# Two-layer hybrid trunk: another order of the projections in the first half of layer 0

## The chip, the cores and the metric

The kernel runs on one core of one Trainium2 chip. The metric is the device time of one execution in microseconds. Engines are named as the profile names them: PE is TensorE (matmuls; PEld its weight loads), DVE is VectorE, ACT is ScalarE, POOL is GpSimd, and SP issues nearly all the DMAs.

## The reference

Two layers run over 2048 prompt tokens and over 8 sample sequences of 16 tokens. Each layer normalises and modulates its input, projects it once into six groups of 512 columns, sends `u` through a state-space branch and `q`, `k`, `v` through stick-breaking attention, gates both branches with SiLU (`z_s`, `z_a`), and projects the joined result onto the residual:

```python
h = rms_norm(x, norm_g) * (1.0 + scale[:, None]) + shift[:, None]
u, z_s, q, k, v, z_a = jnp.split(h @ w_in, [...], axis=-1)
y_s, hr, hi = s5_branch(u, h0_re, h0_im, a_re, a_im, log_dt, ...)   # scan over tokens
y_s = gelu(y_s); y_s = y_s * sigmoid(y_s @ w_glu + b_glu) * silu(z_s)
q = rms_norm(q, q_norm_g); k = rms_norm(k, k_norm_g)                 # per head of 64
y_a = stick_breaking(q, k, v) * silu(z_a)
x = x + gate * (concatenate([y_s, y_a]) @ w_out)
```

Everything is float32. Nothing in the reference orders the six column groups among each other.

## The kernel before

**Tiling.** The 2176 tokens are 17 tiles of 128. They go through a layer in two halves (`TILES`, nine tiles and eight). `proj_half` opens a half: three pairs of buffers `hH`, `hL` hold its normalised input, split into a rounded part and a remainder. `project(st, groups)` then works through column groups one after the other. For each group `weights` loads eight chunks `wr` of 128x512, rounds each on ACT into `wH` (L171) and subtracts the rest into `wL`, on POOL for even chunks and on DVE for odd ones (L172). There are eight `wH` and eight `wL` buffers, so the chunks of one group take the places of the group before it.

**The groups differ in what stands behind PE.**
- `zs` and `za`, the gates, are computed transposed: 12 PSUM tiles `pm` of 128x384, each of 24 matmuls (L726 to L728). A tile leaves through one ACT sigmoid and one DVE product (L731, one operand in PSUM).
- `u`, `v`, `q`, `k` go token tile by token tile: 24 matmuls of 512 columns (L673 to L675) into one `pm`, of which there are two.
- A tile of `q` or `k` goes on through `qk`: two ACT passes, then 16 DVE rows: a sum of squares (L689), twelve narrow steps of 128x8 or so for an inverse root (L194 to L201, all from SBUF to SBUF), a product over 512 columns (L692), then a PE transpose (L696) and the split into `x2` buffers (L706 on ACT, L707 on DVE), which DMAs store to `qT` or `kT`. For `k`, POOL also scales the tile (L698).
- A tile of `v` is stored, read back shifted by one token and subtracted on POOL (L771).

`kn` (three buffers) and `x2` (two) serve all of these; `norm` loads the next half's input into `x2` as well.

**The set-up of the state-space branch** stands between the groups. `ssm_mats(l)` builds matrices in eight batches: on POOL `Gt` (L555), `Et` (L550), `EE` (L552), on DVE `EE` (L551), `GG` (L556, L557), on PE small products (L563) and transposes of `GG` (L573). `ssm_phase(l)` builds a table of rotations by doubling, with DVE and POOL in turn (L444 to L449, L416 to L419). In the first half of layer 0 the chain is `ssm_mats(0)`, both phases, `ssm_mats(1)`, then `ssm_sample(0)`, a serial recurrence on DVE (L1130 to L1133). Each of them takes its buffers from the memory that the one ahead has left, so they follow each other.

**What sets the order.** `build` emits the work in the order of the code. A scheduler then interleaves the instructions of all engines, with earlier emitted work ahead where it is ready by its own estimate of time. The result is one fixed order for each engine and for SP's queue: an instruction that isn't ready holds all that stand behind it on its engine.

Of the kernel before, what the change touches and what calls it, by code (L numbers as in the profile page):

```python
# [44 lines left out]
class Trunk:  # L45
# [6 lines left out]
    def build(self):  # L52
        tc, nc = self.tc, self.nc
        with ExitStack() as es:
# [7 lines left out]
            with ExitStack() as pe:  # L62
                with ExitStack() as px:
# [8 lines left out]
                    st = self.proj_open(pe, 0, 0)  # L72
                    with tc.high_priority(offset=300):
                        self.project(st, ("u",))
                self.project(st, ('q',))
                with ExitStack() as pq:
                    self.stats(self.pool(pq, "stats1", right=True), TILES[1])
                self.ssm_mats(0)
# [2 lines left out]
                    self.ssm_phase(ph, 1)  # L81
                self.ssm_mats(1)
                self.ssm_sample(0)
                self.project(st, ('k', 'v', 'za', 'zs'))
                self.proj_half(st, 1)
                self.project(st, ("u",))
                self.ssm(0)
# [7 lines left out]
            with ExitStack() as pe:  # L95
                st = self.proj_open(pe, 1, 0)
# [5 lines left out]
            with ExitStack() as pe:  # L102
                st = self.proj_open(pe, 1, 1)
# [1180 lines left out]
```

## Time and profile before

| | us |
|---|---|
| median of 3 runs | 3248.16 |
| lowest, highest | 3246.58, 3252.23 |
| the profiled execution | 3246.12 |
| its span, first instruction to last | 3244.3 |

The page of the profile covers the span; 1.8 us of the profiled execution lie around it. Busy time is a union over each engine. Times inside the span count from its start. The stretch that the change touches lies from about 137 us (end of `u`) to 617 us (end of `u` of the second half).

### The profile page before, as it was taken

What the parts mean: (1) busy time and instruction counts of PE and PEld (TensorE: products, weight loads), DVE (VectorE), ACT (ScalarE), POOL (GpSimd) and SP (SyncE); (2) the same over time, 40 slices, a digit from 0 to 9 for tenths busy, and PEclk for the clock granted to TensorE, in tenths of its full rate; (3) what the DMA queues carried; (4) which work ended last, traced back from release to release, by engine and by line L of the source; (5) the groups of instructions that cost most, each with busy time, mean ns of one, the idle gap of its engine ahead of it and who ended that gap; (6) DMA issues with size and microseconds to landing.
All of it is one profiled execution on the core that took longest, in us unless ns stands there. A gap on an engine that the chain in (4) does not pass through costs nothing.

```text
span 3244.3 us, 47167 instructions
## 1 busy us (share of the span) xinstructions
PE 2986.9 (92%) x16902; PEld 2241.4 (69%) x16902; DVE 2233.9 (69%) x3885; ACT 1297.7 (40%) x2646; POOL 710.9 (22%) x468
## 2 busy tenths in 40 slices
PE   6977679899988999999999997899999899999998
PEld 4755578798767657667777785677789565666665
DVE  6699775667476786577885637437474988776865
ACT  4632224334342343365443323463343345343422
POOL 1155664101302022111021003312200202111210
PEclk7999799999999999999999998999999999999999
DMA  6645554465776974343344224757754847444642
GB/s 201 171 145 170 204 174 154 145 184 176 235 267 224 314 228 144 124 139 119 112 139 155 100 65 155 240 193 218 222 173 139 264 127 203 140 129 138 208 136 73
DMA packets 516099, 555.27 MB, mean 171 GB/s; under 512 B 87203, under 2 KB 369491, under 8 KB 515098
## 3 DMA queue, kind: packets, MB, share of 16 engines
q1 hardware_dynamic: 515866, 552.26, 54.3%
q8 instruction: 134, 2.20, 0.3%
q14 instruction: 99, 0.81, 0.1%
HBM read 378.12 MB, written 169.86 MB: 169 GB/s over the span
## 4 chain that ended last, share of the span: by engine, by line
PE 68%; DVE 10%; DMA 5%; issue 4%; ACT 1%; POOL 1%; SPq 1%; DVEq 0%; ACTq 0%; POOLq 0%
PE pt L836 8%; PE po L842 8%; PE pm L673 5%; PE pm L674 5%; PE pm L675 5%; PE pz L819 4%; PE pm L726 3%; PE pz L820 3%; PE pm L728 3%; PE pm L727 3%; PE pm L1243 3%; PE pm L1244 3%; PE pm L1245 3%; DVE u L826 2%; PE pz L990 1%
## 5 line engine op out<-in xcount | busy, mean ns | idle before, releaser
L826 DVE TENSOR_TENSOR_SCAN u<-u 128x512 f32<-128x512 f32 (+3 forms) x640 | 724.2, 1165 | 96.0 <-ACT u L824 92.5
L673 PE MATMUL pm<-wH,hH 128*128 128x512 f32 x1088 | 448.1, 413 | 28.5 <-ACT kn L760 16.3
L674 PE MATMUL pm<-wL,hH 128*128 128x512 f32 x1088 | 444.5, 409 | 10.7 <-DVE wL L172 6.8
L675 PE MATMUL pm<-wH,hL 128*128 128x512 f32 x1088 | 446.4, 411 | 5.9 <-POOL hL L649 4.3
L839 ACT COPY aT<-pt 128x512 f32<-128x512 f32 (+1 forms) x376 | 175.3, 470 | 592.5 <-PE pt L836 568.1
L836 PEld LDWEIGHTS pt<-ident,u 128*128 128x128 f32 x2176 | 240.8, 142 | 233.8 <-issue 194.6
L824 ACT ACTIVATE u<-pz 128x512 f32<-128x512 f32 (+3 forms) x640 | 320.9, 536 | 176.8 <-PE pz L820 61.1
L838 DVE COPY aT<-pt 128x512 f32<-128x512 f32 (+1 forms) x376 | 199.6, 534 | 250.9 <-PE pt L836 241.0
L836 PE MATMUL pt<-ident,u 128*128 128x128 f32 x2176 | 350.8, 285 | 15.5 <-DVE aT L838 11.3
L842 PE MATMUL po<-aT,V 128*64 128x512 f32 (+1 forms) x1504 | 318.4, 506 | 16.4 <-DVE aT L838 7.7
L819 PE MATMUL pz<-K,Q 128*128 128x512 f32 (+2 forms) x640 | 271.6, 425 | 4.8 <-issue 1.6
L726 PE MATMUL pm<-hH,wH 128*128 128x384 f32 (+1 forms) x768 | 259.8, 338 | 17.5 <-DVE kn L731 17.5
L728 PE MATMUL pm<-hH,wL 128*128 128x384 f32 (+1 forms) x768 | 257.3, 336 | 11.0 <-POOL wL L172 8.8
L673 PEld LDWEIGHTS pm<-wH,hH 128*128 128x128 f32 x1088 | 210.6, 194 | 78.9 <-ACT kn L760 17.7
L727 PE MATMUL pm<-hL,wH 128*128 128x384 f32 (+1 forms) x768 | 258.0, 336 | 0.0
L674 PEld LDWEIGHTS pm<-wL,hH 128*128 128x128 f32 x1088 | 210.4, 193 | 60.7 <-DVE wL L172 9.8
L675 PEld LDWEIGHTS pm<-wH,hL 128*128 128x128 f32 x1088 | 210.6, 194 | 58.1 <-POOL hL L649 8.0
L172 POOL TENSOR_TENSOR wL<-wr,wH 128x512 fp32r<-128x512 f32 x96 | 152.3, 1597 | 415.4 <-ACT wH L171 217.3
L820 PE MATMUL pz<-K,Q 128*128 128x512 f32 (+2 forms) x640 | 235.3, 368 | 0.0
L1243 PE MATMUL pm<-owH,mH 128*128 128x512 f32 x512 | 207.4, 405 | 10.0 <-DVE yt L1246 8.8
L1244 PE MATMUL pm<-owL,mH 128*128 128x512 f32 x512 | 205.0, 400 | 4.6 <-DVE owL L172 4.5
L1245 PE MATMUL pm<-owH,mL 128*128 128x512 f32 x512 | 203.6, 398 | 0.0
(373 smaller groups left out, 5211.7 us busy)
## 6 DMA issues: line engine op xcount, KB each, us to landing
wr<-in_w_in_dram SPq DMA_DIRECT2D x192, 256.0 KB
K<-kT SPq DMA_DIRECT2D x184, 256.0 KB
Q<-qT SPq DMA_DIRECT2D x112, 256.0 KB
wm<-in_w_mod_dram SPq DMA_DIRECT2D x24, 1024.0 KB
V<-dv_d SPq DMA_DIRECT2D x92, 256.0 KB
out_dram<-kn SPq DMA_DIRECT2D x68, 256.0 KB
qT<-x SPq DMA_DIRECT2D x64, 256.0 KB
kT<-x SPq DMA_DIRECT2D x64, 256.0 KB
```

What stands on the lines that cost most here:

```text
L673: pe.matmul(ps, hH[:, k, cs], wH[k], start=k == 0, stop=False)
L674: pe.matmul(ps, hH[:, k, cs], wL[k], start=False, stop=False)
L675: pe.matmul(ps, hL[:, k, cs], wH[k], start=False, stop=k == KT - 1)
L726: pe.matmul(ps[:, 0:n], wH[k][:, ws], hH[:, k, 0:n], start=k == 0, stop=False)
L727: pe.matmul(ps[:, 0:n], wH[k][:, ws], hL[:, k, 0:n], start=False, stop=False)
L728: pe.matmul(ps[:, 0:n], wL[k][:, ws], hH[:, k, 0:n], start=False, stop=k == KT - 1)
L819: pe.matmul(pz[:, c0:512], Q1[:, qi], K1[:, 0:N], start=True, stop=False)
L820: pe.matmul(pz[:, c0:512], Q2[:, qi], K1[:, 0:N], start=False, stop=not diag)
L824: sc.activation(u[:, o:512], pz[:, c0:c1], AF.Sigmoid, scale=-0.125)
L826: v.tensor_tensor_scan(un, un, un, 1.0 if diag else carry[hh * 4 + i], ALU.mult, ALU.bypass)
L836: pe.transpose(pTs[hh][:, i * 128:(i + 1) * 128], As[hh][i][:, off + j * 128:off + (j + 1) * 128], ident)
L842: mm = pe.matmul(po[c, s], V1[:, j, c], aTs[hh][:, s], start=diag and j == 0, stop=kc == 0 and j == 3, tile_position=(0, hh * 64))
```

## The change

Two lines of `build` change. In the first half of layer 0 the groups are emitted as `u`, `zs`, `za`, (set-up), `v`, `k`, `q` where they were `u`, `q`, (set-up), `k`, `v`, `za`, `zs`. The number of instructions of each kind stays.

```diff
                     with tc.high_priority(offset=300):
                         self.project(st, ("u",))
-                self.project(st, ('q',))
+                self.project(st, ('zs', 'za'))
                 with ExitStack() as pq:
                     self.stats(self.pool(pq, "stats1", right=True), TILES[1])
                 self.ssm_mats(0)
@@
                 self.ssm_mats(1)
                 self.ssm_sample(0)
-                self.project(st, ('k', 'v', 'za', 'zs'))
+                self.project(st, ('v', 'k', 'q'))
                 self.proj_half(st, 1)
                 self.project(st, ("u",))
```

The scheduler makes of it another order on every engine. On DVE, in the middle of `ssm_mats(0)`, the order before has the normalisation of `q` and `k` (L200, L201, L689) between the set-up's rows:

```order
L556 TENSOR_TENSOR GG_2128<-PWT_1973,Bb1_1982 128x1024
L200 TENSOR_TENSOR rst_1920<-rst_1920,rsm_1919 128x8
L567 TENSOR_TENSOR KK_2139<-KK_2139,Dd_2047 128x16
L557 TENSOR_TENSOR GG_2128<-GG_2128,Gt_2129 128x1024
L201 SCALAR_TENSOR_TENSOR rrq_1918<-rst_1920,rrq_1918 128x8
L551 TENSOR_TENSOR EE_2193<-PWT_1973,C2_1997 128x1088
L689 TENSOR_REDUCE ssq_3118<-x1_3114 128x8
```

The same place of the change, on DVE, has the products of the gate `za` (L731) there:

```order
L551 TENSOR_TENSOR EE_2384<-PWT_2199,C2_2223 128x1088
L567 TENSOR_TENSOR KK_2330<-KK_2330,Dd_2273 128x16
L731 TENSOR_TENSOR kn_1840<-pm_1815,kn_1840 128x384
L731 TENSOR_TENSOR kn_1869<-pm_1844,kn_1869 128x384
L556 TENSOR_TENSOR GG_2354<-PWT_2199,Bb1_2208 128x1024
L551 TENSOR_TENSOR EE_2419<-PWT_2199,C2_2223 128x1088
```

Between the first and the last `EE` or `GG` row of `ssm_mats(0)` DVE had 186 rows of `qk`; now it has none, and 19 products of the gates.

In the middle of `ssm_mats(1)`, on DVE, the order before has gate products and weight remainders:

```order
L557 TENSOR_TENSOR GG_2585<-GG_2585,Gt_2586 128x1024
L551 TENSOR_TENSOR EE_2650<-PWT_2465,C2_2489 128x1088
L731 TENSOR_TENSOR kn_4340<-pm_4315,kn_4340 128x384
L567 TENSOR_TENSOR KK_2596<-KK_2596,Dd_2539 128x16
L172 TENSOR_TENSOR wL_4384<-wr_4381,wH_4383 128x512
L556 TENSOR_TENSOR GG_2620<-PWT_2465,Bb1_2474 128x1024
```

The same place of the change, on DVE, has the normalisation of `k` (two tiles in turn):

```order
L692 TENSOR_TENSOR kn_4049<-kn_4049,rrq_4054 128x512
L199 TENSOR_TENSOR rst_4117<-rrq_4115 128x8
L557 TENSOR_TENSOR GG_2846<-GG_2846,Gt_2847 128x1024
L200 TENSOR_TENSOR rst_4117<-rst_4117,rsm_4116 128x8
L551 TENSOR_TENSOR EE_2841<-PWT_2691,C2_2715 128x1088
L201 SCALAR_TENSOR_TENSOR rrq_4115<-rst_4117,rrq_4115 128x8
L692 TENSOR_TENSOR kn_4110<-kn_4110,rrq_4115 128x512
L556 TENSOR_TENSOR GG_2881<-PWT_2691,Bb1_2700 128x1024
```

Between the first and the last `EE` or `GG` row of `ssm_mats(1)` DVE had no row of `qk` and 13 gate products; now it has 123 rows of `qk` and no gate product.

In SP's queue, at the end of the half, the first loads of the second half's input (`x2_4860` and on) stood in the middle of the stores of `za`:

```order
L163 DMA x2_3942<-v_d0_67 128x512
L163 DMA x2_4860<-in_x_prompt_dram 128x512
L163 DMA wr_4399<-in_w_in_dram 128x512
L163 DMA wr_4405<-in_w_in_dram 128x512
L163 DMA za_d0_75<-kn_4048 128x384
```

In the change SP has them behind the last stores of `q`, whose `x2` buffers they take over:

```order
L163 DMA qT0_63<-x2_4715 128x4x128
L163 DMA qT0_63<-x2_4716 128x4x128
L163 DMA x2_4860<-in_x_prompt_dram 128x512
L163 DMA x2_4875<-in_x_prompt_dram 128x512
L163 DMA x2_4890<-in_x_prompt_dram 128x512
```

They moved from far ahead of the end of the half to its very end.

## Rows read from the trace of the kernel before

**Rows 1.** The page: busy time, and busy tenths in 40 slices of 81 us.
```profile
PE 2986.9 (92%) x16902; PEld 2241.4 (69%) x16902; DVE 2233.9 (69%) x3885; ACT 1297.7 (40%) x2646; POOL 710.9 (22%) x468
...
PE   6977679899988999999999997899999899999998
...
DVE  6699775667476786577885637437474988776865
...
PEclk7999799999999999999999998999999999999999
```

**Rows 2.** Stretches (us): busy PE, PEld, DVE, ACT, POOL; granted clock, DMA share, GB/s.
```profile
137.00:300.00 163.00, 129.10 (x632) 99.41 (x631) 153.79 (x339) 56.62 (x103) 78.51 (x41) 0.93 0.53 163
300.00:395.00 95.00, 67.77 (x263) 54.44 (x264) 84.61 (x113) 20.87 (x27) 67.25 (x47) 0.82 0.52 183
395.00:517.00 122.00, 98.70 (x588) 90.84 (x587) 88.10 (x84) 34.19 (x70) 74.81 (x32) 0.93 0.60 187
517.00:540.00 23.00, 23.00 (x156) 22.33 (x155) 7.34 (x14) 10.28 (x18) 5.02 (x3) 1.00 0.56 171
540.00:617.00 77.00, 65.29 (x327) 47.31 (x326) 57.37 (x94) 43.25 (x90) 17.16 (x12) 0.98 0.32 101
617.00:760.00 143.00, 143.00 (x859) 130.93 (x858) 76.46 (x119) 48.48 (x113) 12.09 (x12) 1.00 0.69 200
```

**Rows 3.** Waits of PE from 137 to 300 us: total, times, longest.
```profile
PE pr L696 <- DVE x L707: 17.5, 4, 10.6
PE pr L696 <- DVE rst L200: 4.9, 1, 4.9
```

**Rows 4.** Waits of PE from 395 to 517 us.
```profile
PE pm L726 <- DVE kn L731: 16.8, 6, 5.3
PE pt L573 <- DVE GG L557: 6.2, 3, 2.7
```

**Rows 5.** Set-up lines, layer 0 then 1: ns min/median/max, first to last start.
```profile
L555 POOL TENSOR_TENSOR Gt<-PWT,Bb x8: 2032/2040/3115, 163.0 to 278.5; 128x1024 f32<-128x1024 f32 x8
L573 PE MATMUL pt<-ident,GG x64: 270/272/330, 201.0 to 290.5; 128*128 128x128 f32 x64
...
L555 POOL TENSOR_TENSOR Gt<-PWT,Bb x8: 2046/2101/3072, 422.8 to 506.1; 128x1024 f32<-128x1024 f32 x8
L573 PE MATMUL pt<-ident,GG x64: 272/273/415, 438.3 to 516.8; 128*128 128x128 f32 x64
```

**Rows 6.** DVE groups from 137 to 292 us: busy, mean ns; idle before.
```profile
L199 DVE TENSOR_TENSOR rst<-rrq 128x8 f32<-128x8 f32 x45 | 15.8, 354 | 0.4
L692 DVE TENSOR_TENSOR kn<-kn,rrq 128x512 f32<-128x512 f32 x14 | 15.6, 1111 | 0.1
```

**Rows 7.** The same groups from 745 to 950 us, no set-up beside them.
```profile
L692 DVE TENSOR_TENSOR kn<-kn,rrq 128x512 f32<-128x512 f32 x16 | 11.0, 690 | 0.6
...
L199 DVE TENSOR_TENSOR rst<-rrq 128x8 f32<-128x8 f32 x48 | 8.7, 185 | 0.8
```

**Rows 8.** Timeline of PE, dense stretches: start, duration of one.
```profile
142.23 0.39 PE L673 MATMUL pm<-wH,hH 128*128 128x512 f32 x1
142.46 0.39 PE L674 MATMUL pm<-wL,hH 128*128 128x512 f32 x1
...
621.05 0.33 PE L728 MATMUL pm<-hH,wL 128*128 128x384 f32 x1
621.22 0.33 PE L727 MATMUL pm<-hL,wH 128*128 128x384 f32 x1
```

**Rows 9.** Set-up groups on PE from 137 to 300 us.
```profile
L573 PE MATMUL pt<-ident,GG 128*128 128x128 f32 x64 | 8.5, 276 | 4.8 <-DVE KK L567 1.9 <-DVE rrq L201 1.8 <-DVE GG L557 1.0
L563 PE MATMUL pz<-EE,Bb 128*32 128x256 f32 x62 | 5.5, 422 | 0.0
```

**Rows 10.** Gate products on DVE from 399 to 518 us.
```profile
L731 DVE TENSOR_TENSOR kn<-pm,kn 128x384 f32<-128x384 f32 x19 | 10.3, 548 | 18.4 <-ACT kn L730 18.3
```

**Rows 11.** Subtractions of `v` on POOL from 300 to 395 us.
```profile
L771 POOL TENSOR_TENSOR x<-x,kn 128x512 f32<-128x512 f32 x7 | 14.2, 2037 | 9.6 <-DMA x<-v_d 9.6
```

## The prediction

> **What bounds the kernel now.** I read the page first, then the stretches by stage, then PE's waits in the stages that the change touches. PE is busy for 92% of the span and its busy tenths are low in the first slices [rows 1]. The stages show where. From 137 to 517 us PE is busy for 129.1 + 67.8 + 98.7 = 295.6 of 380 us, at a granted clock of 0.82 to 0.93; behind it, from 617 us, it is busy for 143 of 143 us at 1.00 [rows 2]. So the first 617 us are where PE can gain or lose, and since it is full afterwards, a shift of the end of this stretch should reach the end of the kernel nearly whole.
>
> Who holds PE there: DVE. It is busy for 153.8 of 163 us up to 300 us and 84.6 of 95 us behind that [rows 2], and PE's waits up to 300 us are on the normalisation of `q` and `k` [rows 3]. From 395 to 517 us PE waits on the products of the gates, 16.8 us, and on the set-up, 6.2 us [rows 4]. DVE is not alone: with POOL it works on a serial chain, ssm_mats(0), the phases, ssm_mats(1), and all of PE's work of this half is over about when that chain is. Its marks: the first POOL step of ssm_mats(0) starts at 163.0 and its last transposes at 290.5; for layer 1 the same marks are 422.8 and 516.8 [rows 5]. The core of the set-up takes 127.5 us with `qk` beside it and 94.0 us with gates beside it.
>
> That difference is the price of company. The 186 rows of `qk` that stand inside the first core cost it 127.5 - 94.0 = 33.5 us, 0.18 us a row. Their own durations fit: a narrow step takes 354 ns there against 185 ns far from any set-up, the wide product 1111 ns against 690 [rows 6, 7].
>
> **The change, part by part.** No work is added or removed. The partners of the chain are exchanged, so each link is costed with its new partner.
>
> *ssm_mats(0) with the gates.* DVE and POOL alone would be done at 163.0 + 94.0 = 257 us. But PE's order now puts the last transposes of ssm_mats(0) behind all of zs, all of za and 129 of v's 216 matmuls. At full clock matmuls start every 0.173 us for 384 columns and 0.23 us for 512 [rows 8], so that is 2 x 288 x 0.173 = 100 us, 129 x 0.23 = 30 us, and for the set-up's own matmuls 16 us (8.5 + 5.5 and two smaller groups of about 2) [rows 9]. From 137 us on this gives 283 us at the least. The gates beside the set-up of layer 1 cost PE 16.8 + 6.2 = 23 us of waits [rows 4]; the upper bound is 306. The DVE queue is as short between two gate products as it was there, but DVE now runs ahead of PE instead of with it, so I take 286 us, near the lower end. Against 290.5 that is -4, with bounds of -7 and +15. The 33.5 us of freed DVE time are thus not passed on: PE's own order takes their place.
>
> *The phases.* They started 10 us behind ssm_mats(0) and took 95 us beside seven subtractions of `v`, 14.2 us of POOL [rows 11]. Five of v's eight subtractions now stand ahead of the phases, and the weights of za are gone from here; the weights of `k` and the normalisation of its first tiles come in, some 50 rows at 0.18 = 9 us. 10 us go, 9 come, part of it in POOL's gaps. I take -3, bounds -12 and +6.
>
> *ssm_mats(1) with k and q.* Its front, 395 to 423 us, is loads from HBM and stays. Its core now holds 123 rows of `qk`: 123 x 0.18 = 22 us on top of 94. Below, if the rows slip into gaps of the chain: 5 us. Above, if none overlaps: a tile's 16 rows take 13 x 0.185 + 3 x 0.69 = 4.5 us far from set-up [rows 7], so 123 rows take 35 us. I take 22, because the row it comes from is the same pair of workloads.
>
> A rule of the Trainium skill bears on that bound: "SBUF — State Buffer", section "Who interferes with whom", says that DVE and GpSimd share one pair of ports as an exclusive lock, held for a whole instruction, which a DVE instruction with two SBUF inputs needs. By that rule alone nothing overlaps and the sum would be 13 us higher; the trace of this kernel shows DVE 88.1 and POOL 74.8 us busy within 122 us [rows 2], so here it agrees only in part. The numbers above don't rest on it.
>
> *What PE has left behind the set-up.* Before, 108 matmuls of zs, 19 us; now 80 of `q`, 18 us: -1.
>
> *The seam to the second half.* The loads of its input took free x2 buffers during za; now they follow q's last stores in SP's queue, and behind those loads wait u's normalisation and PE. What covers it is one more tile of `q` on PE, 24 x 0.23 = 5.5 us, and the sample branch. In the 77 us of u and sample PE is already idle for 11.7 us [rows 2], because DVE runs the sample's recurrence. If that recurrence still ends the stage, the seam costs nothing; without cover, up to 12 us. I take 0 and keep 12 for the range.
>
> *The gate products themselves* keep their price, 0.55 us for a row with an operand in PSUM [rows 10], wherever they stand.
>
> **Sum.** -4 - 3 + 22 - 1 + 0 = +14 us on the profiled execution of 3246.1 us: 3260 us. That execution lies 2 us under the median of the runs, 3248.2, which is less than I can resolve.
>
> **The rivals.**
>
> *Faster: PE fills its holes and the chain doesn't pay.* The gates need little of DVE, and the set-up leaves PE idle for 34 us before 300 us [rows 2]. If ssm_mats(0) ends at 283 (-7), the phases gain 12, and the `qk` rows beside ssm_mats(1) cost only the lower 5 us, the sum is -7 - 12 + 5 - 1 = -15: 3231 us. It decides itself at ssm_mats(1): from about 0.07 us a row downwards the change gains. For it: DVE and POOL do overlap by 41 us of 122 [rows 2]. Against it: the 0.18 us measured in the mirror image. "Perfetto Trace Analysis", section "Optimization Strategy", in the Trainium skill advises to interleave regimes whose busiest engines differ; by that rule this rival is the outcome, and the trace agrees that PE has the holes, but it also shows a second busy pair, DVE with POOL, that no reordering thins out.
>
> *The same: a mirror image.* `qk` leaves one set-up and enters the other; the two prices cancel if ssm_mats(0) passes on some of its gain. With 0.1 us a row (12 us) and -12 from the two first links: 3246 us, give or take 5.
>
> *Much slower: PE starves twice.* Gates wait as before (ssm_mats(0) at 306, +15), `qk` costs 22, the seam some 5: +41, 3287 us. The point is whether zs and za show 20 us of waits again.
>
> That the change does not do what it says can be left out: the orders show the exchange. Later stages are scheduled anew too, with the same work; I allow 5 us either way.
>
> **How the numbers follow.** The forecast, 3253 to 3269, gets 0.40; much slower 0.15; the same 0.20; faster 0.25. What one can tell from no change is about 0.2%, 6.5 us. So slower by more than that 0.55, within it 0.20, faster 0.25. The range leaves out about one in ten on each side: 3228 to 3287.
>
> **What would show it.** Right: the last transposes of ssm_mats(0) start at 280 to 295; PE busy above 90% from 137 to 300; the core of ssm_mats(1) takes 110 to 125 us and ends at 525 to 540; PE is idle longer than now between the phases and the end of `q`; the second half's u ends at 625 to 640. Wrong: a core of ssm_mats(1) under 100 us, or a stretch from 137 us to the end of u shorter than 480 us, speaks for the faster rival; a narrow `qk` step near 185 ns beside ssm_mats(1) means the price per row was mis-sized; an end of u that moves without the end of the kernel means PE was not full behind it.

## The result and the profile after

The changed kernel took 3285.25 us (median of five runs, 3280.93 to 3291.11) against 3248.16 us (five runs, 3241.47 to 3252.39): a ratio of 1.0125, 95% interval 1.0112 to 1.0139, some 36 to 45 us slower. A second measurement beside other kernels gave 1.0117 (1.0096 to 1.0138). The forecast was 3260 us in a range of 3228 to 3287. The sign is right and the range holds the time, but the loss is about three times the forecast.

The page of the changed kernel, busy time and busy tenths in 40 slices (of 82 us; compare [rows 1]). The third slice is fuller than before, the sixth and seventh are emptier, and the clock digits of these two are lower:

```profile
PE 3002.2 (91%) x16902; PEld 2243.4 (68%) x16902; DVE 2240.2 (68%) x3885; ACT 1296.3 (39%) x2646; POOL 718.3 (22%) x468
...
PE   6997667899998999989999998899999799999998
...
PEclk8999788999999999999999999999999999999999
```

The stretches of the changed kernel, cut at the same times as [rows 2] (length, then busy PE, PEld, DVE, ACT, POOL; granted clock, DMA share, GB/s):

```profile
137.00:300.00 163.00, 150.19 (x847) 134.39 (x847) 96.17 (x112) 43.33 (x85) 82.26 (x38) 0.99 0.54 171
300.00:395.00 95.00, 56.12 (x213) 43.97 (x212) 80.80 (x138) 21.53 (x28) 55.33 (x42) 0.77 0.47 167
395.00:517.00 122.00, 82.69 (x381) 62.72 (x381) 118.02 (x193) 31.46 (x58) 75.73 (x36) 0.84 0.54 157
517.00:540.00 23.00, 22.38 (x126) 17.08 (x125) 18.26 (x63) 8.90 (x15) 6.65 (x3) 0.98 0.65 193
540.00:617.00 77.00, 56.21 (x220) 37.60 (x220) 61.97 (x116) 41.88 (x84) 13.89 (x9) 0.84 0.34 107
```

Up to 300 us PE is idle for 12.8 us where it was idle for 33.9. Behind that it pays: 38.9 us against 27.2 up to 395, and 39.3 against 23.3 up to 517. DVE is busy for 118.0 of the 122 us beside `ssm_mats(1)`.

PE from 137 us to the last matmul of the second half's `u` (same columns), in the kernel before:

```profile
137.00:615.50 478.50, 382.36 (x1951) 312.83 (x1950) 389.69 (x640) 163.91 (x304) 241.68 (x134) 0.92 0.52 163
```

and in the changed kernel:

```profile
137.00:640.60 503.60, 390.43 (x1945) 313.99 (x1945) 385.34 (x638) 162.55 (x302) 240.52 (x133) 0.89 0.50 158
```

The same matmuls (a few records are missing) take 25.1 us more: 17.0 us of idle time (96.1 to 113.2) and 8.1 us of busy time, at a mean granted clock of 0.89 instead of 0.92. The idle time is -21.1 up to 300 us, +11.7 up to 395, +16.0 up to 517 and, by what is left of the total, +10.5 from there to the end of `u`.

The chain of the set-up in the changed kernel, as in [rows 5]: layer 0 has one row and layer 1 two (ns min/median/max, first to last start):

```profile
L573 PE MATMUL pt<-ident,GG x64: 270/272/328, 176.0 to 296.6; 128*128 128x128 f32 x64
...
L555 POOL TENSOR_TENSOR Gt<-PWT,Bb x8: 2028/2225/3161, 411.3 to 503.2; 128x1024 f32<-128x1024 f32 x8
L573 PE MATMUL pt<-ident,GG x64: 270/273/448, 421.7 to 521.9; 128*128 128x128 f32 x64
```

The chain is the one of [rows 5]: `ssm_mats(0)`, the phases, `ssm_mats(1)`; its end is the start of the last transpose (L573), and the core of a layer's set-up lies between its first step on POOL (L555) and that. `ssm_mats(0)` ends 6.1 us later than before, the core of layer 1 starts 11.5 us earlier (411.3 against 422.8), takes 110.6 us instead of 94.0 and ends only 5.1 us later. So most of the 25.1 us arises behind the chain. The last products of `u` in the second half (L675, same columns), in the kernel before:

```profile
L675 PE MATMUL pm<-wH,hL x64: 389/393/795, 539.9 to 615.1; 128*128 128x512 f32 x64
```

and in the changed kernel:

```profile
L675 PE MATMUL pm<-wH,hL x64: 388/397/795, 566.5 to 640.2; 128*128 128x512 f32 x64
```

`u` itself is not slower (75.2 and 73.7 us); it begins 26.6 us later. Between the end of the chain and this first row, 21.5 us were lost. The place can be narrowed down further. The last matmul of the last group of the half and the first of `u` (L673) in the kernel before, where a gate is last:

```profile
538.87 0.34 PE L728 MATMUL pm<-hH,wL 128*128 128x384 f32 x1
...
539.40 0.48 PE L673 MATMUL pm<-wH,hH 128*128 128x512 f32 x1
```

and in the changed kernel, where `q` is last:

```profile
541.67 0.39 PE L675 MATMUL pm<-wH,hL 128*128 128x512 f32 x1
...
565.23 0.79 PE L673 MATMUL pm<-wH,hH 128*128 128x512 f32 x1
```

So PE is done with the groups 2.8 us later, 23.6 us lie between them and `u` instead of 0.5, and `u` takes 0.7 us less: 2.8 + 23.0 - 0.7 = 25.1 us. In the gap PE has the last transposes of `q` to do (the last one starts at 558.95), the sample branch's first products (L1119) and the transposes of the first new input tiles (L634). The two longest waits of PE in the changed kernel from 526 to 560 us, then the stretch itself:

```profile
PE pr L696 <- DVE x L707: 5.7, 1, 5.7
PE pz L1119 <- issue: 3.2, 1, 3.2
```

```profile
526.00:560.00 34.00, 23.94 (x122) 17.41 (x120) 26.28 (x72) 16.80 (x24) 8.59 (x5) 0.80 0.72 218
```

In the kernel before, PE had gate matmuls between these small ones and was busy for 23.00 of 23 us at that place, at a clock of 1.00 [rows 2]. Now the last tiles of `q` go through DVE there, PE is busy for 23.9 of 34 us, and the clock is 0.80.

The shift of 25.1 us at the end of `u` is not all: the span grew by 39.2 us (3244.3 to 3283.5). The other 14.1 us come later, where no line of the code was changed.

### The profile page after: what moved, and what is told of

It reads as the page before. It is cut to its first block, busy times and chain, and to the rows that moved or that the text cites. A ratio compares the mean times of both kernels' runs of the same rounds, so it can differ in the third digit from the quotient of the medians.

```text
span 3283.5 us, 47148 instructions
## 1 busy us (share of the span) xinstructions
PE 3002.2 (91%) x16902; PEld 2243.4 (68%) x16902; DVE 2240.2 (68%) x3885; ACT 1296.3 (39%) x2646; POOL 718.3 (22%) x468
## 5 line engine op out<-in xcount | busy, mean ns | idle before, releaser
L674 PE MATMUL pm<-wL,hH 128*128 128x512 f32 x1088 | 445.1, 409 | 25.1 <-POOL wL L172 15.9
L673 PE MATMUL pm<-wH,hH 128*128 128x512 f32 x1088 | 450.0, 414 | 18.1 <-ACT kn L686 7.3
L675 PE MATMUL pm<-wH,hL 128*128 128x512 f32 x1088 | 447.0, 411 | 5.9 <-POOL hL L649 2.6
L842 PE MATMUL po<-aT,V 128*64 128x512 f32 (+1 forms) x1504 | 317.5, 505 | 19.4 <-DVE aT L838 10.2
L819 PE MATMUL pz<-K,Q 128*128 128x512 f32 (+2 forms) x640 | 270.7, 423 | 6.0 <-DMA K<-kT 1.6
L726 PE MATMUL pm<-hH,wH 128*128 128x384 f32 (+1 forms) x768 | 257.4, 335 | 7.2 <-DVE kn L731 5.2
L673 PEld LDWEIGHTS pm<-wH,hH 128*128 128x128 f32 x1088 | 210.9, 194 | 68.7 <-DVE hH L648 9.3
L675 PEld LDWEIGHTS pm<-wH,hL 128*128 128x128 f32 x1088 | 211.0, 194 | 58.3 <-DVE hL L649 6.0
L1243 PE MATMUL pm<-owH,mH 128*128 128x512 f32 x512 | 207.2, 405 | 14.1 <-DVE yt L1246 11.4
```

The lines of the kernel that those rows point to most:

```text
L673: pe.matmul(ps, hH[:, k, cs], wH[k], start=k == 0, stop=False)
L674: pe.matmul(ps, hH[:, k, cs], wL[k], start=False, stop=False)
L675: pe.matmul(ps, hL[:, k, cs], wH[k], start=False, stop=k == KT - 1)
L726: pe.matmul(ps[:, 0:n], wH[k][:, ws], hH[:, k, 0:n], start=k == 0, stop=False)
L819: pe.matmul(pz[:, c0:512], Q1[:, qi], K1[:, 0:N], start=True, stop=False)
L842: mm = pe.matmul(po[c, s], V1[:, j, c], aTs[hh][:, s], start=diag and j == 0, stop=kc == 0 and j == 3, tile_position=(0, hh * 64))
```

## The experiments

Marks of each kernel's profiled execution. "End of u" is the last matmul of `u` in the second half; "idle" is PE's idle time from 137 us to there; "rest" is the span behind it. The ratio is of the timed runs, against the kernel before on the same chip.

| kernel | groups of the first half behind u (bar: the set-up) | end of u | idle | rest | ratio, 95% interval |
|---|---|---|---|---|---|
| before | q, bar, k v za zs | 615.5 | 96.1 | 2629 | 1 |
| after | zs za, bar, v k q | 640.6 | 113.2 | 2643 | 1.0125 (1.0112 to 1.0139) |
| e15_after_again | the same | 639.4 | 112.2 | 2641 | 1.0117 (1.0096 to 1.0138) |
| e1_za_last | zs, bar, v k q za | 639.5 | 113.6 | 2634 | 1.0087 (1.0070 to 1.0104) |
| e2_v_last | zs za, bar, k q v | 633.3 | 105.2 | 2637 | 1.0076 (1.0057 to 1.0094) |
| e3_after_short_qk | as after, 162 rows of qk out | 630.7 | 110.0 | 2611 | 1.0011 (1.0000 to 1.0021) |
| e4_before_short_qk | as before, 162 rows of qk out | 613.5 | 90.9 | 2621 | 0.9975 (0.9960 to 0.9990) |
| e5_k_last | q, bar, v za zs k | 618.8 | 96.9 | 2648 | 1.0061 (1.0041 to 1.0080) |
| e8_v_first | v, bar, q k za zs | 643.5 | 112.3 | 2645 | 1.0144 (1.0111 to 1.0177) |
| e10_v_last_early_x | as e2, input early | 619.4 | 96.1 | 2618 | 0.9993 (0.9978 to 1.0008) |
| e11_after_short_sample | as after, short recurrence | 627.9 | 108.6 | 2620 | 1.0037 (1.0023 to 1.0051) |
| e12_k_before_v | zs za, bar, k v q | 638.1 | 116.4 | 2627 | 1.0082 (1.0062 to 1.0103) |
| e13_before_early_x | as before, input early | 617.4 | 98.9 | 2613 | 0.9973 (0.9962 to 0.9983) |
| e14_q_zs_first_early_x | q zs, bar, k v za, input early | 627.3 | 109.8 | 2615 | 1.0006 (0.9992 to 1.0020) |
| e16_after_early_x | as after, input early | 640.7 | 109.0 | 2638 | 1.0131 (1.0112 to 1.0149) |
| e17_v_k_then_gates | q, bar, v k zs za, input early | 630.7 | 104.2 | 2645 | 1.0113 (1.0098 to 1.0128) |

A single execution lies up to 9.5 us off the median of its kernel (e2_v_last and e5_k_last, 9.5 and 8.7 us above it), so a difference of a few us in "rest" says nothing. The chips differ by up to 10 us too, so where an expectation is held against a time, the ratio is the better measure; 1.0087, for example, is 3276 us beside the 3248 of the first runs.

### Is it the rows of qk? (e3, e4)

```diff
-    def rsqrt(self, pool, y, ss, scale, tag):
+    def rsqrt(self, pool, y, ss, scale, tag, steps=3):
-        for _ in range(3):
+        for _ in range(steps):
-            self.rsqrt(hp, rr, ss, 1.0 / HD, "rq")
+            self.rsqrt(hp, rr, ss, 1.0 / HD, "rq", 0 if l == 0 and half == 0 else 3)
```

> The changed kernel without the three Newton steps of the inverse root for q and k in the first half of layer 0: nine of the sixteen DVE rows of each of 18 tiles are left out, 162 in all, and q and k there are only roughly normalised. Theory (DVE with POOL sets the end of the half): 0.18 us a row is given back, 25 to 35 us, and the time is 3250 to 3260. Rival (the narrow rows hide in DVE's gaps and PE or the loads set the end): 3275 to 3285.

> The same 162 rows left out of the kernel before, where the trace has them beside ssm_mats(0) and the phases. Theory (0.18 us a row beside the set-up, and the chain sets the end): 3248 - 29, so 3215 to 3228 us, as much as the changed kernel gains. Rival (rows cost only where they stand in the tail): 3240 to 3248 here and a gain in the changed kernel alone.

(A tile has thirteen narrow rows, L194 to L201; nine of them are these steps.) By their ratios the two kernels are at 3252 and 3240 us beside 3248: the first in the range of its first theory, the second at the edge of its rival. The same 162 narrow rows are worth 0.0114 of the time in the changed kernel (1.0125 to 1.0011) and 0.0025 in the kernel before. Read by marks this is less than it seems: the end of `u` moves by 9.9 us in the one and by 2.0 us in the other, and the rest comes from the later part, which was ordered anew in both. Without the rows, the set-up of layer 1 in the changed kernel ends no earlier. The row of e3_after_short_qk:

```profile
L573 PE MATMUL pt<-ident,GG x64: 270/273/417, 430.4 to 524.8; 128*128 128x128 f32 x64
```

524.8 against 521.9: what the rows cost did not reach the end of `u` by way of the chain. In e4_before_short_qk the last transposes of `ssm_mats(0)` start at 293.8 (290.5 before), although the core holds 92 rows of `qk` instead of 186. So the difference of 127.5 and 94.0 us, from which the prediction took its price, can't be put down to these rows alone; in e1_za_last, with no row of `qk` in it, this core still takes 106.4 us (164.4 to 270.7).

### Does PE's own order hold ssm_mats(0)? (e1)

```diff
-                self.project(st, ('zs', 'za'))
+                self.project(st, ('zs',))
-                self.project(st, ('v', 'k', 'q'))
+                self.project(st, ('v', 'k', 'q', 'za'))
```

> The order is u, zs, (set-up), v, k, q, za: one gate goes back to the end of the half. Marks of the two traces so far: the last transposes of ssm_mats(1) end at 517 us before and 526 after, the last group of the half at 539 and 560, u of the second half at 616 and 641, the end at 3244 and 3283. Theory (a heavy tail): the change loses because its last group is q, whose every tile waits on DVE, where a gate let PE run at full clock while the set-up ended and the next input was loaded. Then this kernel ends the half at 540 to 548 and takes 3258 to 3270 us. Rival (a longer set-up chain): the rows of qk beside ssm_mats(1), 165 here against 123, cost 0.18 us each wherever za stands; then ssm_mats(1) ends 5 to 10 us later than after and the time is 3280 to 3295 us. Rival (later stages only): 3275 to 3290, whatever stands last.

The transposes of `GG` of layer 0, then of layer 1:

```profile
L573 PE MATMUL pt<-ident,GG x64: 270/272/447, 175.2 to 270.7; 128*128 128x128 f32 x64
...
L573 PE MATMUL pt<-ident,GG x64: 270/273/447, 408.8 to 514.1; 128*128 128x128 f32 x64
```

Yes: with one gate less ahead of the last transposes these start at 270.7 instead of 296.6 (first row). But of the 26 us 8 are left at the end of `ssm_mats(1)` (514.1 against 521.9; its core now holds 165 rows of `qk`) and 1 at the end of `u`, 639.5 against 640.6. An early chain does not make an early half.

Nor does a light group at the end. The last matmuls of `za` (L726) and the first of `u` (L673):

```profile
L726 PE MATMUL pm<-hH,wH x96: 333/334/739, 480.4 to 561.9; 128*128 128x384 f32 x96
...
L673 PE MATMUL pm<-wH,hH x64: 387/393/793, 562.8 to 638.6; 128*128 128x512 f32 x64
```

The gap in front of `u` is closed, but PE is done with the groups at 562 us, where the changed kernel was at 541.7: it now stands idle for 98.0 us up to the end of the chain (91.0 there), beside a DVE that is busy for 203.4 of the 214.1 us from 300 us to there, and `za` is still to come. The tail theory's mark (540 to 548) is missed; 1.0087 (3276 us) lies above its range and in that of the later stages.

### What stands at the end of the half? (e2, e10, e16)

```diff
-                self.project(st, ('v', 'k', 'q'))
+                self.project(st, ('k', 'q', 'v'))
```

> The order is u, zs, za, (set-up), k, q, v: the head of the change, but v, which is light on DVE, at the end. 46 rows of qk stand beside ssm_mats(0) and 65 beside ssm_mats(1), against 0 and 123 after. Theory (a heavy tail): most of the loss goes, 3255 to 3270 us. Rival (the seam: the loads of the second half's input wait for x2 buffers, which v uses too): no better than after, 3278 to 3290. Rival (later stages only): 3275 to 3290.

With `v` at the end PE has done the groups of the first half at 528.5 us, yet `u` ends at 633.3, because one wait, for the first tile of the next input, takes the place of the tail. PE's longest wait from 535 to 640 us:

```profile
PE pr L634 <- ACT x L631: 14.0, 1, 14.0
```

By its ratio (3273 us) the kernel lies between the two ranges that were expected. The wait is the seam of the prediction, in a kernel where nothing covers it. So the next edit loads the first input tile of the second half early, in two buffers of their own:

```diff
+    def early(self, st, p, i):
+        for q in range(2):
+            st.early[1, i, q] = p.tile([128, 512], F32, name="xe", bufs=2)
+            self.dma(st.early[1, i, q], self.x_in(st.l, i)[:, q * 512:(q + 1) * 512])
...
+                    self.early(st, self.pool(pq, "early", right=True), TILES[1][0])
                     self.ssm_mats(1)
...
+                elif (half, i, q) in st.early:
+                    xt = st.early[1, i, q]
```

> Order u, zs, za, set-up, k, q, v as in e2_v_last, with the first tile of the second half's input loaded ahead of ssm_mats(1) into two buffers of its own. In e2_v_last PE stood 14.0 us at one transpose of that input. Seam theory: this wait goes and u of the second half ends 8 to 14 us earlier than in e2_v_last (633), at 619 to 625; the time is 3250 to 3256. Sample theory: u ends with the recurrence of the sample branch, about 105 us behind the end of ssm_mats(1), so PE waits elsewhere, u ends at 628 to 634 and the time stays at 3260 to 3266.

The wait is gone and `u` ends at 619.4, 13.9 us earlier, as the seam theory has it (the time, 3240, is below its range; the rest came out shorter too). That the gain is as long as the wait is in part chance: `u` begins 23.2 us earlier (524.3 against 547.5) and takes longer (95.1 us against 85.8). With the early input and `v` last, the gates ahead of the set-up lose only 3.9 us up to that mark. Is the late input also what the changed kernel waits for? The same edit there:

> The changed kernel with the first tile of the second half's input loaded ahead of ssm_mats(1) into two buffers of its own; q and its rows stay at the end of the half, and the later order is close to that of the changed kernel. If the late input makes the gap in front of u: u of the second half ends at 622 to 632 (changed kernel 640) and the time is 3258 to 3272. If the rows of q on DVE make it: 636 to 642 and 3274 to 3286.

No: `u` ends at 640.7, as in the changed kernel, and the gap in front of it is no shorter: the last matmul of `q` starts at 539.3, the first of `u` at 567.3 (the chain ended 8 us later than in the changed kernel, at 530.0). The rows of `q` on DVE come first there, and the input is covered by them.

Over all kernels the gap, from the last matmul of the last group to the first of `u`, goes with the last group. With `q` or `k` last it is 23.3 to 30.4 us (seven kernels, e5_k_last with 24.1 among them); with a gate last, or `v` and the input early, it is at most 2.4 (eight kernels); e2_v_last has 19.4.

### How much does DVE's other work hold? (e11)

```diff
-            for t in range(DEC):
+            for t in range(DEC if l else 4):
                 prev = hv[:, :, :, :, t - 1] if t else hg
```

> The changed kernel with 4 of the 16 steps of layer 0's sample recurrence: 48 DVE rows between the end of ssm_mats(1) and the end of the second half's u are left out, and the sample's output is not the reference's. Tail theory: u of the second half follows the end of q, so it ends within 5 us of 640 and the time within 6 us of 3277 (the changed kernel against the same runs of before). Sample theory: the recurrence sets the end of u; it ends at 615 to 630 and the time is 3255 to 3267.

The products of `u`:

```profile
L675 PE MATMUL pm<-wH,hL x64: 387/395/791, 564.5 to 627.5; 128*128 128x512 f32 x64
```

`u` ends at 627.9, 12.7 us earlier, inside the window of the sample theory and 7 us below that of the tail theory. But `u` begins only 2.0 us earlier, and the gap in front of it is the same (23.3 us against 23.6). What is shorter is `u` itself, 63.0 us instead of 73.7: the recurrence holds its pace. It does so in the kernel before too (75.2 us), so the recurrence is not what the change lost.

### Is an early chain worth anything? (e5, e8, e17, e14)

The edits of these four stand against the kernel before. e5_k_last:

```diff
-                self.project(st, ('k', 'v', 'za', 'zs'))
+                self.project(st, ('v', 'za', 'zs', 'k'))
```

> Order u, q, set-up, v, za, zs, k: the head of before (99 rows of qk in the core of ssm_mats(0), 46 in that of ssm_mats(1)), but a group with qk at the end of the half instead of a gate, and from the first prompt attention on DVE's and POOL's order is the one of the changed kernel, row for row. Tail theory: what is lost lies behind the set-up, where PE waits for qk's rows; then ssm_mats(1) ends within 6 us of 517, the half ends 8 to 14 us later than 539, and the time is 3255 to 3262. Price-per-row theory (0.13 to 0.18 us for a row beside ssm_mats(1)): ssm_mats(1) ends at 523 to 525, the tail adds nothing: 3246 to 3249. Later-schedule theory: from the end of glu to the end of the kernel it takes 2203 to 2207 us as in the changed kernel, against 2197 before; if that was chance of one execution, 2194 to 2200.

The transposes of layer 1, and the products of `u` in the second half:

```profile
L573 PE MATMUL pt<-ident,GG x64: 270/273/444, 400.4 to 487.1; 128*128 128x128 f32 x64
...
L675 PE MATMUL pm<-wH,hL x64: 387/395/796, 542.3 to 618.4; 128*128 128x512 f32 x64
```

With v in the place of k behind the set-up, the chain of layer 1 is over at 487.1, 29.7 us before the kernel before, and `u` still ends 3.3 us later than there. The rows of `k` at the end leave a gap of 24.1 us here too (516.6 to 540.7), but PE was done with the groups 22 us earlier than in the kernel before. In sum its idle time is the same to 0.8 us. Both theories on the first half missed their mark for `ssm_mats(1)` (517 and 523 to 525). The ratio of 1.0061 belongs to the later part (below).

e8_v_first:

```diff
-                self.project(st, ('q',))
+                self.project(st, ('v',))
...
-                self.project(st, ('k', 'v', 'za', 'zs'))
+                self.project(st, ('q', 'k', 'za', 'zs'))
```

> Order u, v, set-up, q, k, za, zs: 122 rows of qk in the core of ssm_mats(0), 4 in that of ssm_mats(1), the others beside the phases; gates at the end as before; later order nearly that of the changed kernel. Tail theory: a gate at the end costs nothing, so the half ends with the chain: within 6 us of 539, u of the second half within 6 us of 616, and only the later schedule differs: 3240 to 3250. Price-per-row theory: about 160 rows beside the phases at 0.13 to 0.18 us make the phases end 15 us later or more, and ssm_mats(1) ends at 525 or later: 3255 or more.

Neither mechanism held, though the time is on the dearer one's side. The set-up of layer 1 ends as before (515.2), the gates behind it run without a hole, but PE had lost so much up to there (100.6 us of idle time against 84.4, at a clock of 0.84 against 0.90) that it still had gates to do up to 568 us. From 300 to 395 us DVE was busy for 93.8 us and PE for 54.2:

```profile
300.00:395.00 95.00, 54.24 (x230) 42.80 (x229) 93.79 (x211) 25.68 (x34) 52.45 (x39) 0.79 0.39 134
```

e17_v_k_then_gates, beside the early input:

```diff
-                self.project(st, ('k', 'v', 'za', 'zs'))
+                self.project(st, ('v', 'k', 'zs', 'za'))
```

> Order u, q, set-up, v, k, zs, za, with the early input: the head of before, v beside the phases, 25 rows of qk in the core of ssm_mats(1) (before none), two gates at the end; the later order is close to the changed kernel's. If the rows at the end of the half cost the time there, none are here: u of the second half ends within 5 us of 616 or earlier; with the later order some 14 us dearer, 3240 to 3258. If the end of the half costs about 20 us whatever stands there: u at 630 or later, 3260 or more.

The set-up of layer 1 ends at 495.5, 21.3 us before the kernel before, with half of the gates' matmuls still to come. They come too late: PE had stood beside a busy DVE before, and `u` ends 15.2 us later than before: idle 104.2 us, clock 0.87. The numbers are those of the second expectation, but not by its reason: the end of the half cost 2.4 us and not 20. Two of its stretches, beside the phases and behind the chain:

```profile
300.00:395.00 95.00, 54.47 (x198) 42.11 (x197) 89.06 (x172) 23.98 (x32) 51.40 (x31) 0.73 0.45 145
...
496.00:560.00 64.00, 61.89 (x345) 56.85 (x344) 23.80 (x42) 23.47 (x43) 7.81 (x6) 0.97 0.28 89
```

e14_q_zs_first_early_x, beside the early input:

```diff
-                self.project(st, ('q',))
+                self.project(st, ('q', 'zs'))
...
-                self.project(st, ('k', 'v', 'za', 'zs'))
+                self.project(st, ('k', 'v', 'za'))
```

> Order u, q, zs, set-up, k, v, za, with the early input: rows of qk beside ssm_mats(0) and the phases only, none in the core of ssm_mats(1), a gate at the end, and the later order of e10_v_last_early_x. By what the runs so far showed (the phases go with POOL, which has no v there; no row beside ssm_mats(1); no qk at the end): ssm_mats(1) ends at 495 to 517, u of the second half at 600 to 616, and 2617 us behind it: 3217 to 3233. If PE's work and not the chain sets the half: u at 616 to 625 and 3233 to 3245.

The last transposes of layer 1 start at 536.1, 19 us later than before, and `u` ends at 627.3. The expectation of 495 to 517 for the chain was wrong; the time, 1.0006, is saved by the later part.

### Where do the other 14 us come from? (e12, e15, e13)

The scheduler orders the whole program in one go, so a change in layer 0 can turn the order of everything behind it. Over these kernels DVE's rows from the first prompt attention on stand in one of two orders (with small variants) up to the projections of layer 1, and again in one of two in layer 1's second half; e4_before_short_qk alone departs from both further on. Swapping v and k in the changed kernel gives back both orders of the kernel before, but for a few rows:

```diff
-                self.project(st, ('v', 'k', 'q'))
+                self.project(st, ('k', 'v', 'q'))
```

> The changed kernel with v and k swapped: u, zs, za, set-up, k, v, q. q is still last, with 115 rows of qk in the core of ssm_mats(1) (changed kernel: 127), but from the first prompt attention on DVE's and POOL's rows stand in the order of the kernel before. Later-order theory: the end of u of the second half stays late, 630 to 642, and from there to the end it takes 2626 to 2634 us as before (2629), not 2643: 3262 to 3275. If the later loss came with the shift itself or by chance: 2640 to 2646 us behind u, 3275 to 3288. Tail theory beside it: the half ends 10 us or more behind the last transposes of ssm_mats(1) plus what PE had left, near 555 to 560.

> The changed kernel once more, on the chip of the three others. If the split of its loss holds: u of the second half ends at 637 to 644 (before 616) and from there to the end it takes 2638 to 2648 us (before 2629); ratio 1.010 to 1.015. If one of the two was chance of one execution, it comes out more than 6 us away.

e12_k_before_v has a first half that is as late as the changed kernel's (`u` ends at 638.1) and a rest of 2627 us, as the kernel before (2629). The changed kernel once more has 2641. (The half ended at 547 and not at 555 to 560; the chain was later there, 531.3, and the tail behind it shorter.) The sums over the stretches from the end of `u` to the end of the span, in the kernel before:

```profile
sum 2628.50, PE 2502.31 PEld 1853.01 DVE 1762.69 ACT 1054.42 POOL 441.74; mean PE 417.05 PEld 308.84 DVE 293.78 ACT 175.74 POOL 73.62
```

in the changed kernel:

```profile
sum 2642.40, PE 2509.21 PEld 1853.66 DVE 1773.22 ACT 1053.51 POOL 447.22; mean PE 418.20 PEld 308.94 DVE 295.54 ACT 175.59 POOL 74.54
```

and in e12_k_before_v:

```profile
sum 2627.00, PE 2499.95 PEld 1852.03 DVE 1766.41 ACT 1053.87 POOL 441.36; mean PE 416.66 PEld 308.67 DVE 294.40 ACT 175.65 POOL 73.56
```

e5_k_last is the opposite case: the head of the kernel before, `u` 3.3 us late, the later order of the changed kernel row for row, and a rest of 2648 (its execution lies 8.7 us above the median). On e16 and e17 DVE has the same order too, row for row, with 2638 and 2645. So some 14 us of the loss hang on the order that the scheduler happened to choose for later stages and not on what the change does in its place. The work is the same, busy PE differs by 7 to 9 us and idle time by 6 to 7. Two waits of PE in the changed kernel from 1078 to 1466 us, which the kernel before doesn't have in its stretch, are part of it; which exchange of rows makes most of the 14 us stays open:

```profile
PE pm L242 <- DMA wm<-in_w_mod_dram: 3.0, 2, 2.8
PE pm L1243 <- ACT mH L171: 2.5, 1, 2.5
```

The other place with two orders lies in the second half of layer 1. There the kernel before is on the dear side:

> The kernel before with the first tile of the second half's input loaded ahead of ssm_mats(1) into two buffers of its own. The input was no wait there, so the first half stays: u of the second half ends within 5 us of 616. The order from the second half of layer 1 on is that of e10_v_last_early_x, where the stretch from the end of u to the first row of the prompt attention took 312 us instead of 327. Order theory: 312 again and 3226 to 3236. If those 312 us were chance: 3240 to 3250.

The stretch from the end of `u` there to the prompt attention, and the two longest waits of PE in it, in the kernel before:

```profile
2182.00:2508.00 326.00, 312.95 (x1745) 263.05 (x1743) 193.32 (x450) 117.42 (x234) 48.55 (x37) 0.99 0.63 190
```

```profile
PE pz L1036 <- DMA Hi<-HT: 3.5, 2, 2.2
PE pm L673 <- ACT wH L171: 3.2, 1, 3.2
```

and the stretch in e13_before_early_x, which has neither wait:

```profile
2183.40:2495.00 311.60, 308.92 (x1760) 263.39 (x1758) 191.92 (x453) 118.37 (x237) 45.33 (x37) 1.00 0.65 201
```

e13_before_early_x beats both kernels: 0.9973 (0.9962 to 0.9983), 3234 us beside 3242. Its first half gained nothing (`u` at 617.4, 615.5 before); the gain is the other order of layer 1. The two places add up over the kernels. Without this gain the rest is 2638 to 2648 us where the order from the first prompt attention on is the changed kernel's, and 2627 to 2637 where it is that of the kernel before. With it the rest is 2620 and 2634 (e11, e1) in the one case and 2611 to 2618 (e3, e10, e13, e14) in the other.

## The prediction, step by step

The forecast at the end of `u` was -4 - 3 + 22 - 1 + 0 = +14 us, and nothing behind it. The marks give +6.1 - 17.6 + 16.6 + 20.0 = +25.1 us, and +14.1 behind it.

**ssm_mats(0): -4 forecast, +6 measured.** The last transposes start at 296.6, inside the bounds of 283 to 306, just outside the sign of 280 to 295. The reason held: PE's own order sets this time (e1: 270.7 with one gate less), and PE was busy for 150 of 163 us, above the 90% named. It came 14 us above the 283 us of pure work, where 3 were forecast: a term of the sum that was too small, by 10 us.

**The phases: -3 forecast.** The core of layer 1 starts 11.5 us earlier, although `ssm_mats(0)` ended 6.1 us later. So the phases with the loads behind them gave 17.6 us, more than the lower bound of -12. The exchange of partners was right in its sign and too small; the subtractions of `v` on POOL fell from 14.2 us [rows 11] to 7.1, and the rest of the gain was not taken apart. The row of the changed kernel, 300 to 395 us:

```profile
L771 POOL TENSOR_TENSOR x<-x,kn 128x512 f32<-128x512 f32 x5 | 7.1, 1410 | 10.3 <-DMA x<-v_d 10.3
```

**ssm_mats(1): +22 forecast, +16.6 measured.** The core took 110.6 us, at the lower edge of the 110 to 125 named; 16.6 / 123 rows is 0.13 us a row. It ended at 521.9, three us before the window of 525 to 540. The price was in the right region: over the other kernels this core takes 93.1 us with 4 rows of `qk` in it (e8), 98.4 with 46 (e5), 106.4 with 65 (e2) and 122.9 with 165 (e1), so 0.13 to 0.18 us a row. But its derivation falls with e4: fewer rows beside `ssm_mats(0)` did not bring its end forward. And the prediction read the shared lock of "SBUF — State Buffer", section "Who interferes with whom" in the Trainium skill, against sums of busy time, which can't test it. The trace agrees with the lock for the narrow rows: those that wait for POOL count as busy (last section).

So the chain was forecast 15 us late and was 5 us late. The forecast's sign rested on it and came true by other terms, which is in part luck.

**What PE has left, and the seam: -1 and 0 forecast, some +20 measured.** This is the step that failed. Its count of PE's matmuls was good: `q` was over 19.8 us behind the chain, where 18 were forecast. But it let `u` follow at once. A tile of `q` is over only when 16 rows on DVE and four transposes behind them are, while DVE also owes the sample branch and the next input, and PE had little else to do meanwhile: 23.6 us passed between the last matmul of `q` and the first of `u`, and 0.5 behind a gate. The late input, for which the prediction kept 12 us, is not the cause (e16: no gain from an early one), though it is ready to take over as soon as the rows are gone (e2: 14.0 us).

The gap goes with the last group in fifteen of the sixteen kernels (e2's is that of the input). That it would have been saved by another last group is not shown: a gate there closed it, and the time came back as idle time further ahead (e1). Only `v` last with an early input brought `u` close to the kernel before (e10).

**The sum over a chain.** Behind this stands a premise: "all of PE's work of this half is over about when that chain is". e1, e5 and e17 end the chain 8, 30 and 21 us earlier than their counterparts and gain 1, -3 and -15 us at the end of `u`. PE's idle time up to that mark follows the end of `u` far better: 91 to 99 us in the five kernels that reach it by 620 us, 104 to 116 in the eleven that need 627 or more. This is a ledger and not a cause, since the end of `u` is 137 us plus PE's busy and idle time; the busy time, 380 to 395 us, moves it too, with the clock. The right ledger was there in [rows 2]: PE's idle time by stretch, with the place where each group of DVE rows goes. By it, the change took 21 us of holes out of the head and put 38 us behind it.

**Later stages: 0, give or take 5; +14 measured.** The prediction said that they are scheduled anew and priced that at 5 us either way. The runs show a rest between 2611 and 2648 us for the same later work (single executions), so a fair allowance was about 15 us either way. e12 has this term at zero with nearly the same first half, so it is a matter of luck, and no reason in the prediction could have had it.

**The rivals.** "Much slower" gave 3287 and the time came out at 3285, but not by its mechanism: it needed 20 us of waits of zs and za and 5 at the seam; the gates' products made 4.5 us up to 300 us, and the seam some 20. The right number there has the wrong reason. "Faster" was half right: PE does fill its holes in the head. It failed behind the set-up. The rule of "Perfetto Trace Analysis", section "Optimization Strategy" in the Trainium skill, to interleave regimes whose busiest engines differ, was followed in the head, where the trace agrees with it (12.8 us of idle time for 33.9); the regime that was bound by DVE then stood without company further on, PE's idle time grew by 38 us there, and the kernel got 1.25% slower.

**The shift of the end of u should reach the end of the kernel** held where the later order is nearly that of the kernel before: in e12 `u` ended 22.6 us later and the span 21.3. In the changed kernel the 14 us came on top, and `u` ended at 640.6, just outside the sign of 625 to 640.

## What to carry to other kernels

Where the last group of a stage has a heavy follower on a second engine, price the time from its last matmul to the next group's first, and not its matmuls alone: it was 23 to 30 us here, and next to nothing behind a light group. But light work kept for the end pays only if it isn't missed earlier: e1, e8, e14 and e17 ended with a gate and were 12 to 28 us late all the same, because PE stood idle beside a busy DVE further ahead. Cost a reordering by the idle time of the bound engine, stretch by stretch, not by the end of a side chain, since a chain that ends earlier shortens nothing if the holes only move. And where one scheduler orders the whole program, measure a second kernel with nearly the same edit before a difference of half a per cent is put down to the edit: later stages alone moved by up to 37 us here, of which up to 9.5 can be a single execution's.

## What was not expected of the hardware

The granted clock moved with the place of the waits. From 395 to 517 us PE waited a dozen times in the changed kernel, up to 5.8 us, was busy for 82.7 of 122 us and was granted 0.84 in the mean, between full speed (2.4 GHz) and the lower level (1.2 GHz); with gates in that place it had 0.93 [rows 2]. From 137 to 300 us, where it now ran nearly without a break, the clock rose from 0.93 to 0.99. The longest waits of PE from 395 to 526 us in the changed kernel:

```profile
PE pr L696 <- DVE rst L199: 11.2, 3, 5.5
PE pm L674 <- DVE rrq L201: 5.8, 1, 5.8
PE pr L696 <- DVE KK L567: 5.7, 1, 5.7
```

Up to the end of `u` PE's busy time grew by 8.1 us at the lower clock, a third of the loss there; the prediction had no term for it.

The narrow rows of `qk` took even longer beside a set-up than [rows 6] showed: in the changed kernel two kinds of 128x8 steps took 432 and 625 ns in the mean on DVE from 409 to 521 us, and 375 and 282 ns from 526 to 560 us, where POOL was busy for 8.6 of 34 us (the first kind 185 ns far from any set-up [rows 7]). The groups of the first stretch, then of the second:

```profile
L200 DVE TENSOR_TENSOR rst<-rst,rsm 128x8 f32<-128x8 f32 x23 | 14.2, 625 | 0.2
...
L199 DVE TENSOR_TENSOR rst<-rrq 128x8 f32<-128x8 f32 x24 | 10.2, 432 | 0.1
...
L199 DVE TENSOR_TENSOR rst<-rrq 128x8 f32<-128x8 f32 x12 | 4.5, 375 | 0.1
...
L200 DVE TENSOR_TENSOR rst<-rst,rsm 128x8 f32<-128x8 f32 x12 | 3.4, 282 | 0.4
```

The means mix two kinds of rows. From 300 to 560 us the changed kernel has 108 rows of these two kinds. The 84 that meet no instruction of POOL take 170 ns at most; of the 24 that meet one, 15 take much longer, up to 4.5 us, and each of these ends 21 to 26 ns behind an instruction of POOL. One of them, with the instruction of POOL that it meets and the next row of DVE:

```profile
541.46 1.54 POOL L172 TENSOR_TENSOR wL<-wr,wH 128x512 fp32r<-128x512 f32 x1 [3.03 <-ACT wH L171]
541.48 1.54 DVE L200 TENSOR_TENSOR rst<-rst,rsm 128x8 f32<-128x8 f32 x1
...
543.05 0.17 DVE L201 SCALAR_TENSOR_TENSOR rrq<-rst,rrq 128x8 f32<-128x8 f32 x1
```

So a long row is a short one that stood until POOL was done, and the profile counts its wait as busy. A part of DVE's 118.0 busy us is such waiting. The mean length of a row is thus no measure of what it costs the chain: at 432 to 625 ns a row the core of `ssm_mats(1)` grew by 0.13 us a row.
